# A fifth pair of seven products per gate and up block, a first block in the same form, and part of the weight sums on GpSimd

## The chip, the core and the metric

The kernel runs on one core of a Trainium2 chip. Its engines have a queue of instructions each and run beside each other: TensorE (PE in the profile; its weight loads are PEld), VectorE (DVE), ScalarE (ACT), GpSimd (POOL) and SyncE (SP), which here only issues loads. An instruction waits on semaphores, and everything behind it on its engine waits with it. The metric is the time of one execution in microseconds; the median of several runs is compared.

## What is computed

One layer of a hybrid block for 256 tokens of width 2048, in float32: differential attention and a Conformer convolution side by side, an output projection, then a SwiGLU feed-forward network. The change is in the second half:

```
h  = h + mixed @ w_out                      # 2048 x 2048
hn = rms_norm(h, norm2_g)
a  = hn @ w_gate                            # 2048 x 5632
bu = hn @ w_up                              # 2048 x 5632
h  = h + (silu(a) * bu) @ w_down            # 5632 x 2048
```

`rms_norm` divides each token's row by its root mean square and multiplies by a gain for each column.

## The kernel before

**Three products for one.** Float32 accuracy is made of the faster fp32r matmuls: an operand x is split into `hi` (x rounded, by ScalarE) and `lo` (x - hi, by VectorE), and hi·hi + lo·hi + hi·lo are added up in PSUM. Weights are split as they arrive: a *chunk* is two k-tiles (128 rows each) of 512 columns. `load_chunk` (SP) fetches it into a `raw` buffer, `round_chunk` casts it to `whi`, `split_chunk` makes `wlo` on VectorE. For some chunks (`BY_DMA`) `wlo` is made without VectorE: ScalarE writes -hi and GpSimd issues a DMA that adds the raw weights to it. With tokens in two halves of 128, a chunk takes 2 x 2 x 3 = 12 matmuls of 128x512.

**Seven products for eight.** The FFN's gate and up matrices share their left operand, so a *pair* of k-tiles, two token halves and the two matrices form a 2x2 by 2x2 block product, which a Winograd-like scheme does in seven products: 21 matmuls instead of 24. It costs sums. Of the activations, once: `make_forms` builds seven `forms` (`fhi`, `flo`). Of the weights, for every pair: `round_pair` makes four sums `t` (tile `wt`, three VectorE instructions, L1049 to L1051) and casts the raw weights, `split_pair` casts the sums (L1055) and makes the remainders `wlb` (L1058, 1536 columns) and `wlt` (L1059, 2048 columns). Of the results, once a block: `bank_sums` (L1186 to L1193) adds up the seven PSUM banks when the block's last pair is multiplied, and `block_done` (L1209, L1214) adds the last two when the block is, and multiplies silu(gate) by up. In the profile's names `q` is a PSUM bank, `sum` what is made of it, `wb` a pair's raw weights, `ps_a`, `ahi`, `alo` the transposed result.

**The blocks.** The 5632 hidden columns are 11 blocks of 512. Block 0 is computed with plain chunks, gate and then up, since the activations' forms are made beside it; blocks 1 to 10 have four pairs (NS = 4) and four chunks each of gate and up. Blocks come in groups of 4, 4 and 3 (`FGROUPS`), and after each group a `down_pass` in two halves multiplies its hidden columns by `w_down`, with pairs of its own and forms made by `make_down_forms` (tiles `dsums`, `dlo`, `dls`).

**What sets the order.** The program is emitted chunk by chunk. `ORDER` says in which order a block's units stand: s is a pair, g a gate chunk, u an up chunk. `run_chunks` rounds units three ahead of the one multiplied and splits two ahead (`HI_AHEAD`, `LO_AHEAD`). Between units it resumes generators (`resume`), such as `products_done`, which runs the bank sums, so these stand on VectorE between the remainders of units to come. Buffers bound how far ahead the engines run: `RAW_BUFS` = 5 for `raw`, two for `wb`, `wh`, `wlb` and `wlt`, three for `whi` and `wlo`, one for `wt`. The eight PSUM banks of a block are all that there are.

## Time and profile before

| | |
|---|---|
| runs | 1032.35, 1032.80, 1032.89 us; median 1032.8 |
| span of the profiled execution, first to last instruction | 1030.8 us |
| instructions | 13034, among them 4642 matmuls |
| mean granted TensorE clock | 1.000 |
| loads and stores | 238.64 MB, 232 GB/s |
| VectorE, casts' remainders L335 / L1059 / L1058 | 250.4 / 139.8 / 106.8 us |
| ScalarE, casts L326 / L1055 / L1052 | 264.2 / 116.8 / 89.8 us |
| DMAs issued by GpSimd for `wlo` | 48, 7.1 us to landing |

Of the profiled execution only its span is given; it stands beside a median that is 2.0 us above it. A row of a timeline has the start in the span, the length, the engine, line and operation, out<-in, and in brackets the idle time before it and what ended that. A row of a group has the count, the busy time, the mean of one in ns, and the idle time. A row of a window has its stretch, and for PE, PEld, DVE, ACT and POOL the busy time and count, then the clock.

### The profile page before, as it was taken

What the parts mean: (1) busy time and instruction counts of PE and PEld (TensorE: products, weight loads), DVE (VectorE), ACT (ScalarE), POOL (GpSimd) and SP (SyncE); (2) the same over time, 40 slices, a digit from 0 to 9 for tenths busy, and PEclk for the clock granted to TensorE, in tenths of its full rate; (3) what the DMA queues carried; (4) which work ended last, traced back from release to release, by engine and by line L of the source; (5) the groups of instructions that cost most, each with busy time, mean ns of one, the idle gap of its engine ahead of it and who ended that gap; (6) DMA issues with size and microseconds to landing.
All of it is one profiled execution on the core that took longest, in us unless ns stands there. A gap on an engine that the chain in (4) does not pass through costs nothing.

```text
span 1030.8 us, 13034 instructions
## 1 busy us (share of the span) xinstructions
PE 1025.7 (100%) x4642; PEld 849.4 (82%) x4642; DVE 929.2 (90%) x1128; ACT 643.4 (62%) x786; POOL 102.7 (10%) x146
## 2 busy tenths in 40 slices
PE   9999999999999999999999999999999999999998
PEld 8888888888888888888888888888888888888887
DVE  6899999999765699999999898989999989889998
ACT  7644656665756675676666556667757556657562
POOL 0300112111000000100102101101001111010020
PEclk9999999999999999999999999999999999999999
DMA  9757555544466677997989799889798979897776
GB/s 338 254 194 258 190 184 164 158 169 166 141 215 214 197 262 222 282 265 210 254 259 272 251 257 270 258 234 262 228 269 255 285 207 283 247 267 218 226 200 174
DMA packets 116448, 238.64 MB, mean 232 GB/s; under 512 B 7840, under 2 KB 9120, under 8 KB 116384
## 3 DMA queue, kind: packets, MB, share of 16 engines
q1 hardware_dynamic: 105216, 203.58, 59.3%
q0 software_dynamic: 10880, 34.08, 17.0%
q8 instruction: 36, 0.59, 0.2%
q14 instruction: 28, 0.23, 0.1%
q10 hardware_dynamic: 288, 0.16, 0.1%
HBM read 204.24 MB, written 9.44 MB: 207 GB/s over the span
## 4 chain that ended last, share of the span: by engine, by line
PE 100%; POOL 0%; DVE 0%; issue 0%; POOLq 0%
PE acc L365 11%; PE acc L366 11%; PE acc L371 11%; PE q L1097 11%; PE q L1103 11%; PE q L1098 11%; PE q L1078 9%; PE q L1077 9%; PE q L1076 9%; PE ps_a L898 1%; PE ps_s L712 1%; PE ps_o L782 1%; PE ps_warm L164 0%; PE ps_h L846 0%; PE ps_qk L693 0%; PE ps_at L802 0%
## 5 line engine op out<-in xcount | busy, mean ns | idle before, releaser
L326 ACT CAST whi<-raw 128x1024 fp32r<-128x1024 f32 (+1 forms) x256 | 264.2, 1043 | 143.8 <-PE acc L366 86.6
L335 DVE TENSOR_TENSOR wlo<-raw,whi 128x1024 fp32r<-128x1024 f32 (+1 forms) x208 | 250.4, 1214 | 38.2 <-ACT whi L326 38.0
L1055 ACT CAST wh<-wt 128x2048 fp32r<-128x2048 f32 x61 | 116.8, 1915 | 109.9 <-DVE wt L1051 109.7
L1059 DVE TENSOR_TENSOR wlt<-wt,wh 128x2048 fp32r<-128x2048 f32 x61 | 139.8, 2291 | 19.8 <-ACT wh L1055 19.7
L1097 PE MATMUL q<-whi,chi 128*128 128x512 f32 x320 | 125.2, 391 | 0.0
L1098 PE MATMUL q<-whi,clo 128*128 128x512 f32 x320 | 124.6, 389 | 0.0
L365 PE MATMUL acc<-whi,xhi 128*128 128x512 f32 x312 | 124.1, 398 | 0.0
L366 PE MATMUL acc<-whi,xlo 128*128 128x512 f32 x312 | 122.2, 392 | 0.0
L1076 PE MATMUL q<-wh,fhi 128*128 128x512 f32 x280 | 109.8, 392 | 0.0
L1077 PE MATMUL q<-wh,flo 128*128 128x512 f32 x280 | 109.0, 389 | 0.0
L1058 DVE TENSOR_TENSOR wlb<-wb,wh 128x1536 fp32r<-128x1536 f32 x61 | 106.8, 1751 | 1.0 <-ACT wh L1052 1.0
L572 DVE SCALAR_TENSOR_TENSOR y<-upad,cw,y 128x256 f32<-128x256 f32 x240 | 101.6, 490 | 0.0
L330 POOL DMA_DIRECT2D wlo<-raw x48 | 41.5, 865 | 555.7 <-ACT wlo L329 286.3
L1052 ACT CAST wh<-wb 128x1536 fp32r<-128x1536 f32 x61 | 89.8, 1472 | 1.0 <-DMA wb<-in_w_down_dram 1.0
L1103 PE MATMUL q<-wlo,chi 128*128 128x512 f32 x320 | 85.7, 390 | 0.0
L371 PE MATMUL acc<-wlo,xhi 128*128 128x512 f32 x312 | 85.2, 394 | 0.0
L1049 DVE TENSOR_TENSOR wt<-wb 128x1024 f32<-128x1024 f32 x61 | 74.4, 1220 | 0.0
L1097 PE MATMUL q<-whi,ahi 128*128 128x512 f32 x182 | 71.0, 390 | 0.0
L1098 PE MATMUL q<-whi,alo 128*128 128x512 f32 x182 | 70.9, 389 | 0.0
L1103 PEld LDWEIGHTS q<-wlo,chi 128*128 128x128 f32 x320 | 60.0, 188 | 12.7 <-DMA wlo<-raw 0.3
L1097 PEld LDWEIGHTS q<-whi,chi 128*128 128x128 f32 x320 | 60.1, 188 | 12.3
L1098 PEld LDWEIGHTS q<-whi,clo 128*128 128x128 f32 x320 | 60.1, 188 | 12.2
(260 smaller groups left out, 1850.5 us busy)
## 6 DMA issues: line engine op xcount, KB each, us to landing
raw<-in_w_in_dram SPq DMA_DIRECT2D x78, 512.0 KB, 4.6
raw<-in_w_gate_dram SPq DMA_DIRECT2D x48, 512.0 KB, 5.0
raw<-in_w_up_dram SPq DMA_DIRECT2D x48, 512.0 KB, 5.3
wlo<-raw POOLq DMA_DIRECT2D x48, 512.0 KB, 7.1
raw<-in_w_down_dram SPq DMA_DIRECT2D x46, 512.0 KB, 6.2
wb<-in_w_down_dram SPq DMA_DIRECT2D x42, 512.0 KB, 5.9
wb<-in_w_up_dram SPq DMA_DIRECT2D x40, 512.0 KB, 4.4
wb<-in_w_gate_dram SPq DMA_DIRECT2D x40, 512.0 KB, 5.5
```

What stands on the lines that cost most here:

```text
L326: act.copy(c["hi"], c["raw"])
L335: dve.tensor_tensor(c["lo"], c["raw"], c["hi"].bitcast(F32), ALU.subtract)
L365: pe.matmul(ps[m], xhi[:, ms], hi[:, j, :], start=c["first"] and j == 0, stop=False)
L366: pe.matmul(ps[m], xlo[:, ms], hi[:, j, :], start=False, stop=False)
L371: pe.matmul(ps[m], xhi[:, ms], lo[:, j, :], start=False, stop=c["last"] and j == nk - 1)
L1055: act.copy(c["hi"][:, :SUMMED], c["t"])
L1059: dve.tensor_tensor(lot, c["t"], c["hi"][:, :SUMMED].bitcast(F32), ALU.subtract)
L1076: pe.matmul(ps, hi, c["hi"][:, w], start=bool(first), stop=False)
L1077: pe.matmul(ps, lo, c["hi"][:, w], start=False, stop=False)
L1097: pe.matmul(ps, xs[i][0][:, ms], hi[:, i, :], start=i == 0 and bool(c["first"].get(qs[m])), stop=False)
L1098: pe.matmul(ps, xs[i][1][:, ms], hi[:, i, :], start=False, stop=False)
L1103: pe.matmul(sum_bank(c, qs[m]), xs[i][0][:, ms], lo[:, i, :], start=False, stop=i == 1 and bool(c["last"].get(qs[m])))
```

## The change

- **A fifth pair.** `PAIRS` lists pairs of k-tiles: (0,8), (1,9), (2,10), (3,11) and now (4,5). Blocks 1 to 10 use all five, and three chunks each of gate and up are left (tiles 6, 7, 12 to 15). `ORDER` becomes "sgsgsgsusuu", for block 1 "gsgsgssusuu".
- **Block 0** takes the form of the others with four pairs, in the order "gugusgsgssuu"; the plain code for it (`silu_done`, `up_done`) goes. Its PSUM pools are exchanged (`swap`).
- **Row factors later.** The activations are no longer multiplied by the rows' factor `rstd2` ahead of the forms (four VectorE instructions and two transposes go); it is applied to the gate's sums, by the Silu's scale and by one more copy (`products_done`). So `make_forms` starts after the third of the four output-projection blocks, and `out_done` writes `rows` and the remaining tiles' `chi` and `clo` straight from PSUM.
- **GpSimd sums.** The three instructions for a pair's sums `t` are in `first_sums(c, engine)`. At the end of `bank_sums`, `sums_aside` lets GpSimd make them for the next pair that is not rounded yet, if its raw weights were loaded and the pair ahead of it is split. `bank_sums` also releases one bank earlier.
- **Halves.** `split_pair` casts `t` in two instructions of 1024 columns and makes `wlt` in two.
- `RAW_BUFS` goes from 5 to 4. Memory is laid out in new pools (`keep`, `late`, `edge`).

```diff
-RAW_BUFS = 5
+RAW_BUFS = 4
...
-NS = 4
-REST = [k for k in range(KD) if k % HK >= NS]
+PAIRS = [(0, 8), (1, 9), (2, 10), (3, 11), (4, 5)]
+NS = len(PAIRS)
+REST = [k for k in range(KD) if not any(k in p for p in PAIRS)]
...
-BY_DMA = dict(g=TWOS[:2], u=TWOS[1::2])
-ORDER = "sggsggsuusuu"
-FIRST_ORDER = "gsggsgsuusuu"
+BY_DMA = dict(g=TWOS[:2], u=TWOS[1:])
+ORDER = "sgsgsgsusuu"
+ORDERS = {1: "gsgsgssusuu"}
+NS0 = 4
+TWOS0 = [*PAIRS[NS0:], *TWOS]
+ORDER0 = "gugusgsgssuu"
+DOWN_ORDER = "sggsggsuusuu"
...
     def round_pair(c):
...
-        c["t"] = t = fp.tile([P, 4, N], F32, tag="wt", name="wt")
         c["hi"] = fp.tile([P, 7, N], F32R, tag="wh", name="wh", bufs=2)
-        dve.tensor_tensor(t[:, 2:4], b[:, 1:3], b[:, 0:1].to_broadcast([P, 2, N]), ALU.subtract)
-        dve.tensor_tensor(t[:, 1], b[:, 1], t[:, 3], ALU.add)
-        dve.tensor_tensor(t[:, 0], t[:, 1], b[:, 3], ALU.subtract)
+        if "t" not in c:
+            first_sums(c, dve)
         act.copy(c["hi"][:, SUMMED:], b[:, 1:])
 
+    def first_sums(c, engine):
+        b = c["b"]
+        c["t"] = t = ffn["pool"].tile([P, 4, N], F32, tag="wt", name="wt")
+        engine.tensor_tensor(t[:, 2:4], b[:, 1:3], b[:, 0:1].to_broadcast([P, 2, N]), ALU.subtract)
+        engine.tensor_tensor(t[:, 1], b[:, 1], t[:, 3], ALU.add)
+        engine.tensor_tensor(t[:, 0], t[:, 1], b[:, 3], ALU.subtract)
+
+    def sums_aside():
+        pairs = [c for c in chunks if c.get("kind") == "s"]
+        n = next((n for n, c in enumerate(pairs) if not c.get("rounded")), None)
+        if n and "b" in pairs[n] and "lo" in pairs[n - 1]:
+            first_sums(pairs[n], pool)
+
     def split_pair(c):
-        act.copy(c["hi"][:, :SUMMED], c["t"])
...
-        dve.tensor_tensor(lob, c["b"][:, 1:], c["hi"][:, SUMMED:].bitcast(F32), ALU.subtract)
-        dve.tensor_tensor(lot, c["t"], c["hi"][:, :SUMMED].bitcast(F32), ALU.subtract)
+        for i in (2, 0):
+            act.copy(hi[:, i : i + 2], t[:, i : i + 2])
+        rest(lob, b[:, 1:], hi[:, SUMMED:])
+        for i in (2, 0):
+            rest(lot[:, i : i + 2], t[:, i : i + 2], hi[:, i : i + 2])
...
         dve.tensor_tensor(u3, q[Q7], u2, ALU.add)
+        dve.tensor_tensor(w1, q[Q2], w1, ALU.add)
         dve.tensor_tensor(w4, q[Q5], u3, ALU.add)
         dve.tensor_tensor(u2, q[Q5], u2, ALU.add)
-        dve.tensor_tensor(w1, q[Q2], w1, ALU.add)
         dve.tensor_tensor(u3, q[Q4], u3, ALU.add)
+        sums_aside()
...
-        for t in g:
-            act.activation(t, t, AF.Silu)
+        for m, t in enumerate(g):
+            act.activation(t, t, AF.Silu, scale=rstd2[m])
+            act.activation(t, t, AF.Copy, scale=rstd2[m])
```

VectorE from the last bank sum of block 1 to pair 2 of block 2, before (`sum`, `q`: the block's sums and banks; `wt`, `wlb`, `wlt`: pair 2's sums and remainders):

```order
L1193 TENSOR_TENSOR sum_4002<-q_3709,sum_4002 128x512
L1209 TENSOR_TENSOR sum_4001<-q_3760,sum_4001 128x512
L1209 TENSOR_TENSOR sum_4003<-q_3918,sum_4003 128x512
L1214 TENSOR_TENSOR sum_4001<-sum_4001,sum_4000 128x512
L1214 TENSOR_TENSOR sum_4003<-sum_4003,sum_4002 128x512
L1049 TENSOR_TENSOR wt<-wb 128x1024
L1050 TENSOR_TENSOR wt<-wb,wt 128x512
L1051 TENSOR_TENSOR wt<-wt,wb 128x512
L1058 TENSOR_TENSOR wlb<-wb,wh 128x1536
L1059 TENSOR_TENSOR wlt<-wt,wh 128x2048
```

The same place now:

```order
L1199 TENSOR_TENSOR sum_4007<-q_3723,sum_4007 128x512
L1217 TENSOR_TENSOR sum_4006<-q_3775,sum_4006 128x512
L1217 TENSOR_TENSOR sum_4008<-q_3942,sum_4008 128x512
L1222 TENSOR_TENSOR sum_4006<-sum_4006,sum_4005 128x512
L1222 TENSOR_TENSOR sum_4008<-sum_4008,sum_4007 128x512
L1064 TENSOR_TENSOR wlb<-wb,wh 128x1536
L1064 TENSOR_TENSOR wlt<-wt,wh 128x1024 x2
```

Pair 2's three sums have left VectorE at this place, and `wlt` is made in halves. They stand on GpSimd, among the DMAs that it issues for `wlo`; from the row factor on, its queue reads:

```order
L234 TENSOR_TENSOR rstd_145<-rsq,neghalf 128x2
L340 DMA wlo<-raw 128x1024 x6
L1040 TENSOR_TENSOR wt<-wb 128x1024
L1041 TENSOR_TENSOR wt<-wb,wt 128x512
L1042 TENSOR_TENSOR wt<-wt,wb 128x512
L340 DMA wlo<-raw 128x1024 x4
```

The first set belongs to pair 2 of block 2; there are 14 in all, for pair 2 of blocks 2 to 10 and of five halves of down passes. Before, no sums stood there. VectorE from the last bank sums of block 0 to pair 2 of block 1, now:

```order
L1198 TENSOR_TENSOR sum_3664<-q_3490,sum_3664 128x512
L1199 TENSOR_TENSOR sum_3665<-q_3346,sum_3665 128x512
L1064 TENSOR_TENSOR wlb<-wb,wh 128x1536
L1064 TENSOR_TENSOR wlt<-wt,wh 128x1024 x2
L1217 TENSOR_TENSOR sum_3664<-q_3386,sum_3664 128x512
L1217 TENSOR_TENSOR sum_3666<-q_3389,sum_3666 128x512
L1222 TENSOR_TENSOR sum_3664<-sum_3664,sum_3663 128x512
L1222 TENSOR_TENSOR sum_3666<-sum_3666,sum_3665 128x512
L345 TENSOR_TENSOR wlo<-raw,whi 128x1024
L1040 TENSOR_TENSOR wt<-wb 128x1024
L1041 TENSOR_TENSOR wt<-wb,wt 128x512
L1042 TENSOR_TENSOR wt<-wt,wb 128x512
```

Here pair 1's remainders stand behind the bank sums and ahead of the closing sums, and pair 2's sums stay on VectorE. Before, block 0 had no bank sums, and in their place stood two products of silu and up (L883).

## The prediction

> **What bounds the kernel now.** I read the shares of the engines first, then the slices, then the chain of waits.

> ```profile
> PE 1025.7 (100%) x4642; PEld 849.4 (82%) x4642; DVE 929.2 (90%) x1128; ACT 643.4 (62%) x786; POOL 102.7 (10%) x146
> PE   9999999999999999999999999999999999999998
> DVE  6899999999765699999999898989999989889998
> PE 100%; POOL 0%; DVE 0%; issue 0%; POOLq 0%
> ```

> TensorE is busy in every slice and is the whole chain: nothing else ever ends last. So a matmul removed is time removed, as long as the matmuls left are still fed in time. VectorE is the engine to fear, at nine tenths from slice 17 on, the half with the FFN.

> What a matmul costs, and the length of a block, from the timeline of TensorE around block 2, and from the windows:

> ```profile
> 456.62 0.39 PE L1077 MATMUL q<-wh,flo 128*128 128x512 f32 x1
> ...
> 461.16 0.39 PE L1097 MATMUL q<-whi,chi 128*128 128x512 f32 x1
> ...
> 466.60 0.39 PE L1076 MATMUL q<-wh,fhi 128*128 128x512 f32 x1
> 466.60:508.00 41.40, 41.40 (x188) 34.31 (x187) 39.87 (x41) 27.95 (x27) 3.05 (x4) 1.00 0.80 231
> ```

> Between the first two rows lie 20 starts: 4.54 / 20 = 0.227 us a matmul. A pair (21) holds TensorE 4.77 us, a chunk of two whole k-tiles (12) 2.72. At 461.16 the pairs of the block are done (its "half"), at 466.60 the next block begins: two chunks, 5.44 us, during which VectorE sums the banks. The window is one block, 180 matmuls and 8 transposes: (41.40 - 40.86) = 0.5 us for the transposes, at a clock of 1.00.

> What VectorE does across that seam, from its timeline (start, length):

> ```profile
> 457.14 1.75 DVE L1058 TENSOR_TENSOR wlb<-wb,wh 128x1536 fp32r<-128x1536 f32 x1
> 458.81 2.29 DVE L1059 TENSOR_TENSOR wlt<-wt,wh 128x2048 fp32r<-128x2048 f32 x1
> 461.13 0.69 DVE L1188 TENSOR_TENSOR sum<-q,sum 128x512 f32<-128x512 f32 x1
> 461.93 0.69 DVE L1189 TENSOR_TENSOR sum<-q,sum 128x512 f32<-128x512 f32 x1
> ...
> 465.12 0.68 DVE L958 TENSOR_TENSOR dsums<-raw_act,dsums 128x512 f32<-128x512 f32 x1
> 466.34 1.29 DVE L1209 TENSOR_TENSOR sum<-q,sum 128x512 f32<-128x512 f32 x2 [0.54 <-PE q L1103]
> 467.55 1.29 DVE L1214 TENSOR_TENSOR sum<-sum,sum 128x512 f32<-128x512 f32 x2
> 468.75 1.22 DVE L1049 TENSOR_TENSOR wt<-wb 128x1024 f32<-128x1024 f32 x1
> 470.00 0.69 DVE L1050 TENSOR_TENSOR wt<-wb,wt 128x512 f32<-128x512 f32 x1
> 470.73 0.69 DVE L1051 TENSOR_TENSOR wt<-wt,wb 128x512 f32<-128x512 f32 x1
> 471.34 0.68 DVE L962 TENSOR_TENSOR dlo<-raw_act,dhi 128x512 fp32r<-128x512 f32 x1
> 471.94 1.75 DVE L1058 TENSOR_TENSOR wlb<-wb,wh 128x1536 fp32r<-128x1536 f32 x1
> 474.43 2.29 DVE L1059 TENSOR_TENSOR wlt<-wt,wh 128x2048 fp32r<-128x2048 f32 x1 [0.73 <-ACT wh L1055]
> ...
> 477.23 2.35 DVE L335 TENSOR_TENSOR wlo<-raw,whi 128x1024 fp32r<-128x1024 f32 x2
> 479.50 1.22 DVE L1049 TENSOR_TENSOR wt<-wb 128x1024 f32<-128x1024 f32 x1
> 477.72 0.39 PE L1078 MATMUL q<-wlt,fhi 128*128 128x512 f32 x1
> ```

> Starts overlap lengths, so I price by start to start: six bank sums 4.0 us (461.13 to 465.12), the four sums that close a block 2.4, a pair's three first sums 2.6 (468.75 to 471.34), its wlb 1.67, a 1024-wide remainder 1.13 (two in 2.27), a small op 0.6. The last two rows give the spare time: pair 2's remainders end at 476.72, TensorE wants the first at 477.72. **One microsecond of lead**, because VectorE must wait for the block's end (466.34) before it can start pair 2. It rebuilds the lead later in the block.

> **The change part by part.**

> 1. Matmuls. Block 0: 192 become 180. Ten blocks: 180 become 177. 12 + 30 = 42 fewer, 42 x 0.227 = 9.5 us; two transposes of the row factors go too, 0.1, and I count 9.7.

> 2. VectorE's new load. Without GpSimd a pair costs 2.6 + 1.67 + 2 x 1.13 = 6.5 us; one whose sums GpSimd made costs 3.9. In a block with five pairs TensorE takes 177 x 0.227 + 0.5 = 40.7 us. VectorE between two sets of bank sums, from the instructions in their order: 46.4 for block 0 to 1 (4.0 bank sums, 2.4 closing, 3.9 pair 1's remainders, five pairs of 6.5, three chunks' remainders 3.4), 40.5 to block 2, 44.8 to 3 (two chunks' remainders, four pairs of 6.5, one of 3.9, ten small ops), about 37 and 34 (down), 39.8, 38.7, 40.5, 44.8 (to 7), and under 40.7 from there. So it is above TensorE in three places only, by 5.7, 4.1 and 4.1, 13.9 us together: that is the loss if no lead carries over; if all of it carries, the loss is nothing. Both ends are kept.

> 3. Block 1, step by step, from block 0's end on TensorE = 0 (its half is -5.4). VectorE: bank sums to -1.4, pair 1's remainders (they stand behind the bank sums now) to 2.5, wanted at 2.72 + 0.45 = 3.2: in time. The closing sums to 4.9, one chunk's remainder 6.0, pair 2 to 12.6. TensorE, in the order g s g s, wants it at 2.72 + 4.77 + 2.72 + 0.45 + 0.25 (transposes) = 10.9: **1.7 us stall**. Pair 3 to 20.2, wanted at 20.3. Pair 4 follows pair 3 with no chunk between (order ...ss...): ready at 26.8, wanted at 25.1, **1.7**. Pair 5: 0.2. Sum 3.6 us.

> 4. A steady block (2, 5, 6, 8, 9), start = 0. Closing sums end at 2.1 (at 3.1 in block 2, entered 1 us late). Pair 2, summed by GpSimd, 6.1, wanted at 4.77 + 2.72 + 0.45 = 7.9. Pair 3 12.6 against 15.4, pair 4 20.3 against 22.9, pair 5 28 to 29.5 against 30.4. No stall.

> 5. Blocks 3 and 7 carry ten more small ops, 6 us: in block 3, entered 1.3 us late, pair 4 is ready at 24.1 against 23.4 and pair 5 0.7 late again, 1.4 us in all; in block 7, entered nearly on time, 0.5. Then the bank sums begin 4.7 us after the half; TensorE takes the banks back one by one, the last of them 4 us into the next block, so that wait stays off its path. Block 10 and the six down passes: nothing. Losses: 3.6 + 1.4 + 0.5 = 5.5 us.

> 6. Casts in halves. The second remainder now needs only one half-cast; this row and the 0.73 above show the wait that goes:

> ```profile
> L1059 DVE TENSOR_TENSOR wlt<-wt,wh 128x2048 fp32r<-128x2048 f32 x61 | 139.8, 2291 | 19.8 <-ACT wh L1055 19.7
> ```

> 19.8 / 61 = 0.3 us a pair, which I left out of the 6.5. If the wait stayed, block 1 would lose about 1.3 us more, and blocks 3 and 7 as much each: 4 us.

> 7. GpSimd's sums. No row shows one of this size; the nearest are small, with VectorE's beside them:

> ```profile
> 36.40 0.46 POOL L200 TENSOR_TENSOR gcsq<-rt,gb 128x128 f32<-128x128 f32 x1
> 36.82 0.32 POOL L201 TENSOR_TENSOR gcsq<-rt,gb 128x64 f32<-128x64 f32 x1
> 37.10 1.30 POOL L202 TENSOR_TENSOR gcsq<-rt,gb 128x64 f32<-128x64 f32 x1
> 39.07 0.32 POOL L202 TENSOR_TENSOR gcsq<-rt,gb 128x64 f32<-128x64 f32 x1
> 36.90 1.32 DVE L335 TENSOR_TENSOR wlo<-raw,whi 128x1024 fp32r<-128x1024 f32 x1 [1.71 <-ACT whi L326]
> ```

> Starts are 0.42 apart for 128 columns and 0.28 for 64: 2.2 ns a column and 0.14. 1024 + 512 + 512 columns: an estimate of 4.9 us, against 2.6 on VectorE as the lower end. It begins when pair 1's remainders end, about the half, and so ends 0.5 us ahead of the block's end: hidden, since pair 2's remainders start 2.1 after it. If that cover goes, see the second rival. Queued behind these sums on GpSimd stand the DMA issues of the next wlo; the first has 14 us until its matmul.

> The same rows show a clash. L202 takes 1.30 beside a VectorE op on two SBUF tensors that ends at 38.22, and 0.32 alone; the VectorE op takes 0.1 longer than the 1.22 at 479.50. Beside ops that read PSUM there is none:

> ```profile
> 126.08 1.01 POOL L671 TENSOR_TENSOR fk<-ssq,neghalf 128x4 f32<-128x4 f32 x1
> 126.46 0.41 DVE L682 TENSOR_TENSOR t<-acc,gcsk 128x256 f32<-128x256 f32 x1
> L671 POOL TENSOR_TENSOR fk<-ssq,neghalf 128x4 f32<-128x4 f32 x4 | 4.0, 1009 | 0.3
> ```

> L671 keeps its mean. The bank sums read PSUM, so the sums on GpSimd and those on VectorE lie side by side; I take no clash in the sum. [...]

> 8. The rest. The forms of the hidden rows are made under the last output-projection block and under block 0's four whole chunks (4 x 2.72 us of cover); a miss costs at most one chunk, 2.7. Loads keep their bytes: 28 chunks of one matrix become 28 halves of pairs on SP's queue. Four raw buffers instead of five: a block now has 6 such chunks, not 8.

> ```profile
> raw<-in_w_gate_dram SPq DMA_DIRECT2D x48, 512.0 KB, 5.0
> ```

> A load of 5.0 us against the four chunks (10.9 us) that four buffers hold: nothing, with up to 2 us in the opening, where loads come as fast as they are used. ACT gets some 45 us more at 62%: off the path.

> Sum: 1030.8 - 9.7 + 5.5 = 1026.6 us of span. The runs' median, 1032.8, is 2.0 above the span; with that, **1028.6 us**.

> **Rivals.** (a) Every surplus is absorbed: 1032.8 - 9.7 = 1023.1. For it: in the profile of before VectorE has leads that grow inside each block and TensorE never waits. Against: block 1's stall comes after a wait that empties the lead.

> (b) The sums on GpSimd slip from under the bank sums. The mechanism is the clash above; the place is pair 2 of the nine blocks 2 to 10; it decides when the last sum ends later than 4.0 us after the block's start (7.9 less the 3.9 of pair 2's remainders, which then wait behind the sums), 4.5 us later than I think. Each further microsecond costs nine; if VectorE waits all 4.9 us from 2.1 on, pair 2 is ready at 10.9 against 7.9: 9 x 3.0 = 27, 1056. I price it at 1.5 us a block: 1028.6 + 13.5 = 1042. [...]

> (c) No lead carries: 1032.8 - 9.7 + 13.9 = 1037.0, slower. It holds if VectorE waits at each block for the half and the end as now, and pays its surplus on top. Against: block 2's 40.5 is under 40.7, and the down passes return 4 to 6 us each.

> (d) Nothing is gained since the losses equal 9.7: 1032.8, between forecast and (c). That GpSimd's sums would not be taken is ruled out by the order, which has 14 sets of them.

> **How the numbers follow.** Forecast 0.50, with its own range of 1026 to 1031.5; (a) 0.18; (b) 0.10; (c) 0.12; (d) 0.10. The predicted time is the forecast's. The range takes in (a) and (c): 1022.5 to 1037. A measurement can tell 0.2%, 2.1 us: faster is below 1030.7. Faster: 0.18 and 0.42 of the forecast's half, 0.60; slower: (b) and most of (c), 0.20; same: 0.20.

> **What would show it.** Right: the idle time of TensorE stands before matmuls on wlt (pairs 2 and 4) of block 1, 3 to 4 us, and some 2 us in blocks 3 and 7, ended by VectorE; GpSimd's first sum lasts about 2.4 us and starts beside the bank sums. Step 1 is right if TensorE has 42 matmuls fewer at 0.227. Wrong: TensorE idle before pair 2 of every block, or GpSimd rows far above 2.4; or a chain of waits that goes through ACT or a DMA, which the sum holds off the path.

## The result, and the profile after

The changed kernel takes **1041.7 us** (median of four runs, 1039.2 to 1045.9) against 1032.6: ratio 1.0092, 95% interval 1.0079 to 1.0106. It is slower by 9 us where 4 less were forecast, and above the range. The profiled execution took 1043.9 us, 2.2 above the median, its span 1042.1; the losses below are those of this one execution. From the page, the engines and the chain; then the view of waits for TensorE (waiting line, what it waited for, us in total, times, longest):

```profile
PE 1023.0 (98%) x4598; PEld 842.1 (81%) x4598; DVE 950.9 (91%) x1202; ACT 689.5 (66%) x876; POOL 180.2 (17%) x191
PE 13%; DMA 1%; DVE 0%; issue 0%
```

```profile
PE q L1107 <- DMA wlo<-raw: 6.7, 7, 1.9
PE ps_h L867 <- DVE h L849: 2.9, 2, 2.7
PE q L1082 <- DVE wlt L1064: 2.0, 2, 1.3
PE ps_warm L174 <- POOL neghalf L168: 1.4, 1, 1.4
PE acc L408 <- ACT whi L336: 1.2, 1, 1.2
PE acc L381 <- DVE wlo L345: 1.1, 1, 1.1
```

44 instructions of TensorE are gone, the 42 matmuls and two transposes, so the gain of step 1 is there. What ate it is new: the largest wait is for a DMA, on remainders made beside VectorE (`wlo`, L1107), which the prediction had named as a sign that it is wrong; only the third line is the wait that was forecast. A wait's row counts the engine's empty time; what TensorE loses is a little more. Taking every start-to-start of two matmuls, less 0.227 us, I get 10.3 us lost in the span of before and 30.4 now. The 20.1 us more are:

| lost by TensorE, us | before | now |
|---|---|---|
| remainders by DMA (L1107) | 0 | 8.0 |
| transposes of h ahead of block 0 (L867) | 0 | 3.3 |
| a remainder ahead of block 0 (L381) | 0 | 1.3 |
| matmuls at half clock | 0 | 3.3 |
| pairs 2 and 4 of block 1 (L1082) | 0 | 2.3 |
| the first 230 us | 5.4 | 6.1 |
| the rest, 0.02 to 0.3 us each | 4.9 | 6.1 |

1030.8 - 9.6 + 20.1 = 1041.3, near the 1042.1 measured.

**The start of block 0.** VectorE, then TensorE, timelines:

```profile
341.56 1.22 DVE L1040 TENSOR_TENSOR wt<-wb 128x1024 f32<-128x1024 f32 x1
342.81 0.69 DVE L1041 TENSOR_TENSOR wt<-wb,wt 128x512 f32<-128x512 f32 x1
343.54 0.69 DVE L1042 TENSOR_TENSOR wt<-wt,wb 128x512 f32<-128x512 f32 x1
344.14 1.22 DVE L345 TENSOR_TENSOR wlo<-raw,whi 128x1024 fp32r<-128x1024 f32 x1
345.28 1.28 DVE L849 TENSOR_TENSOR h<-h,acc 128x512 f32<-128x512 f32 x2
```

```profile
342.28 1.07 PE L1107 MATMUL q<-wlo,hhi 128*128 128x512 f32 x4
346.02 0.33 PE L867 MATMUL ps_h<-ident,h 128*128 128x128 f32 x1 [2.67 <-DVE h L849]
```

The first pair's sums (L1040 to L1042) are emitted one step ahead of the additions to h (L849) that the transposes wait for. And TensorE's gap has an aftermath. The windows of this gap, behind it, and behind the longest wait on a DMA (stretch; PE, PEld, DVE, ACT, POOL; the clock; then the DMA engines' share and GB/s):

```profile
343.00:346.40 3.40, 0.68 (x3) 0.14 (x1) 3.37 (x5) 0.41 (x1) 0.14 (x1) 1.00 0.68 247
346.90:350.30 3.40, 3.40 (x11) 2.72 (x10) 2.17 (x5) 2.24 (x5) 1.40 (x3) 0.50 0.80 293
449.30:452.70 3.40, 3.40 (x9) 2.63 (x8) 3.40 (x4) 1.99 (x2) 0.00 (x0) 0.50 0.93 304
```

For 3.4 us behind each wait the granted clock is 0.50 and a matmul takes 0.427 instead of 0.227 us: 8 matmuls, 1.6 us lost twice.

**A steady block.** Block 2, whose second gate chunk has its remainder by DMA. ScalarE, GpSimd, then VectorE and SyncE's queue, timelines:

```profile
432.74 0.73 ACT L1209 ACTIVATE sum<-sum,rstd 128x512 f32<-128x512 f32 x1
433.37 1.99 ACT L1057 CAST wh<-wt 128x1024 fp32r<-128x1024 f32 x2
435.27 1.05 ACT L336 CAST whi<-raw 128x1024 fp32r<-128x1024 f32 x1
436.22 1.06 ACT L339 ACTIVATE wlo<-raw 128x1024 fp32r<-128x1024 f32 x1
```

```profile
428.50 2.73 POOL L1040 TENSOR_TENSOR wt<-wb 128x1024 f32<-128x1024 f32 x1
431.31 1.30 POOL L1041 TENSOR_TENSOR wt<-wb,wt 128x512 f32<-128x512 f32 x1
432.69 1.30 POOL L1042 TENSOR_TENSOR wt<-wt,wb 128x512 f32<-128x512 f32 x1
437.80 0.88 POOL L340 DMA_DIRECT2D wlo<-raw  x1 [3.82 <-ACT raw_act L913]
```

```profile
435.06 1.75 DVE L1064 TENSOR_TENSOR wlb<-wb,wh 128x1536 fp32r<-128x1536 f32 x1
436.93 0.37 SPq L1022 DMA_DIRECT2D wb<-in_w_up_dram  x1
437.34 0.47 SPq L1022 DMA_DIRECT2D wb<-in_w_gate_dram  x1
```

And TensorE, whose matmul ahead of the last row starts at 446.19:

```profile
446.19 0.39 PE L1102 MATMUL q<-whi,clo 128*128 128x512 f32 x1
448.49 1.44 PE L1107 MATMUL q<-wlo,chi 128*128 128x512 f32 x4 [1.91 <-DMA wlo<-raw]
```

It wants this `wlo` at 446.4 and gets it at 448.49. GpSimd's queue is not what delays it: it stood idle for 3.82 us. The copy on ScalarE (L339) stands behind the two half-casts of pair 2's sums (L1057), and these behind the scaling of the gate's sums (L1209). ScalarE does not wait for GpSimd here: the sums are done at 433.99, and the second half-cast starts at 434.32 without idle time before it. And the transfer enters 0.5 to 0.9 us behind a pair's loads, the first of which starts 0.12 us after VectorE's `wlb` (done at 436.81) has set their buffer free. The DMA view of 436.9 to 438.2 gives the times to landing:

```profile
wb<-in_w_up_dram SPq DMA_DIRECT2D x1, 512.0 KB, 3.8
wb<-in_w_gate_dram SPq DMA_DIRECT2D x1, 512.0 KB, 5.3
wlo<-raw POOLq DMA_DIRECT2D x1, 512.0 KB, 10.6
raw<-in_w_up_dram SPq DMA_DIRECT2D x1, 512.0 KB, 9.5
```

10.6 us, against a median of 7.1 before. It moves nothing for the first 4.6 us: in the DMA view of 438.0 to 442.4 the only queue with packets is SyncE's (packets, MB, share of the 16 DMA engines):

```profile
q1 hardware_dynamic: 596, 1.15, 94.7%
```

Over 9 us there were 3 of 48 such transfers before, and 14 of 51 now.

### The profile page after: what moved, and what is told of

Read it like the earlier page. It is cut to its first block, busy times and chain, and to the rows that moved or that the text cites. A ratio compares the mean times of both kernels' runs of the same rounds, so it can differ in the third digit from the quotient of the medians.

```text
span 1042.1 us, 13141 instructions
## 1 busy us (share of the span) xinstructions
PE 1023.0 (98%) x4598; PEld 842.1 (81%) x4598; DVE 950.9 (91%) x1202; ACT 689.5 (66%) x876; POOL 180.2 (17%) x191
## 5 line engine op out<-in xcount | busy, mean ns | idle before, releaser
L336 ACT CAST whi<-raw 128x1024 fp32r<-128x1024 f32 (+1 forms) x228 | 237.6, 1044 | 133.6 <-PE acc L376 66.0
L345 DVE TENSOR_TENSOR wlo<-raw,whi 128x1024 fp32r<-128x1024 f32 (+1 forms) x177 | 214.9, 1218 | 46.7 <-ACT whi L336 42.3
L1057 ACT CAST wh<-wt 128x1024 fp32r<-128x1024 f32 x150 | 155.0, 1052 | 83.8 <-DVE wt L1040 56.9
L1064 DVE TENSOR_TENSOR wlt<-wt,wh 128x1024 fp32r<-128x1024 f32 x150 | 176.5, 1218 | 0.7 <-ACT wh L1057 0.7
L1080 PE MATMUL q<-wh,fhi 128*128 128x512 f32 x378 | 148.0, 392 | 0.0
L1081 PE MATMUL q<-wh,flo 128*128 128x512 f32 x378 | 147.6, 390 | 0.0
L1064 DVE TENSOR_TENSOR wlb<-wb,wh 128x1536 fp32r<-128x1536 f32 x75 | 131.3, 1751 | 5.7 <-ACT wh L1035 5.6
L1082 PE MATMUL q<-wlt,fhi 128*128 128x512 f32 x216 | 85.0, 393 | 2.0 <-DVE wlt L1064 2.0
L381 PE MATMUL acc<-wlo,xhi 128*128 128x512 f32 x312 | 84.9, 393 | 0.0
L1081 PEld LDWEIGHTS q<-wh,flo 128*128 128x128 f32 x378 | 71.4, 189 | 15.0
L1080 PEld LDWEIGHTS q<-wh,fhi 128*128 128x128 f32 x378 | 71.4, 189 | 14.7
L1040 DVE TENSOR_TENSOR wt<-wb 128x1024 f32<-128x1024 f32 x61 | 74.4, 1220 | 4.2 <-DMA wb<-in_w_gate_dram 2.7
L1107 PE MATMUL q<-wlo,chi 128*128 128x512 f32 x264 | 71.7, 393 | 3.3 <-DMA wlo<-raw 3.3
## 6 DMA issues: line engine op xcount, KB each, us to landing
raw<-in_w_in_dram SPq DMA_DIRECT2D x78, 512.0 KB, 3.9
wb<-in_w_up_dram SPq DMA_DIRECT2D x54, 512.0 KB, 4.2
wb<-in_w_gate_dram SPq DMA_DIRECT2D x54, 512.0 KB, 6.0
wlo<-raw POOLq DMA_DIRECT2D x51, 512.0 KB, 7.4
raw<-in_w_down_dram SPq DMA_DIRECT2D x46, 512.0 KB, 6.0
wb<-in_w_down_dram SPq DMA_DIRECT2D x42, 512.0 KB, 5.8
raw<-in_w_gate_dram SPq DMA_DIRECT2D x34, 512.0 KB, 4.4
raw<-in_w_up_dram SPq DMA_DIRECT2D x34, 512.0 KB, 7.2
```

The costliest lines, as they stand in the source:

```text
L336: act.copy(c["hi"], c["raw"])
L345: dve.tensor_tensor(c["lo"], c["raw"], c["hi"].bitcast(F32), ALU.subtract)
L1057: act.copy(hi[:, i : i + 2], t[:, i : i + 2])
L1064: dve.tensor_tensor(lo, raw, h.bitcast(F32), ALU.subtract)
L1080: pe.matmul(ps, hi, c["hi"][:, w], start=bool(first), stop=False)
L1081: pe.matmul(ps, lo, c["hi"][:, w], start=False, stop=False)
```

## The experiments

Theories: A, GpSimd's sums themselves make the remainders late; B and C, the loads of five pairs come in lumps and a transfer that enters behind a lump is late; and, for the whole, that VectorE has no lead left, so that what is mended at one place is lost at the next. Times are medians; before was 1032.6 or 1032.7 beside every one. Of the views of waits only the lines that bear on the argument are shown.

**1. Sums back on VectorE**, in `sums_aside`:

```diff
-            first_sums(pairs[n], pool)
+            pass
```

> The changed kernel with the 14 sets of GpSimd sums put back on VectorE; nothing else differs. Theory A (the sums on GpSimd make the remainders by DMA late: the copies on ScalarE stand behind casts that wait for GpSimd, and the DMA issues stand behind the sums): the flights of 9.5 to 11 us of the wlo transfers that are issued beside or right after a set go back to about 7, the idle time before the matmuls on such a wlo goes from 6.7 us and more to under 1.5; in exchange VectorE has 14 x 2.6 = 36 us more, some 2.4 us a block above TensorE in nine blocks, so up to 20 us stand before matmuls on wlt: 1040 to 1052 us. Theory B (the transfers are late because the loads of five pairs with four raw buffers come in bunches, whoever makes the sums): flights stay at 9.5 to 11 where loads are bunched and the waits on wlo stay at 6 us or more beside the wlt stalls: 1048 to 1058.

1054.8 us (ratio 1.0214, 1.02 to 1.0227), in the range of theory B. Its waits:

```profile
PE q L1082 <- DVE wlt L1064: 7.2, 13, 1.3
PE q L1107 <- DMA wlo<-raw: 3.0, 4, 1.8
PE ps_h L867 <- DVE h L849: 2.9, 2, 2.7
PE ps_a L906 <- DVE sum L1222: 1.7, 7, 0.3
PE q L1080 <- DVE sum L1217: 1.6, 2, 0.8
```

GpSimd's sums are worth 13 us to this kernel. The flights separate: the first gate chunk's stay long (9.7 and 10.3 us in blocks 2 and 3, as with the sums on GpSimd), the second's fall from 10.6 and 9.1 to 6.2 and 6.0, and there the transfer entered at 437.16, 0.6 us ahead of the pair's loads (437.77). Counted from the first of block 1's bank sums, the transfer enters at 10.0 us here and at 9.7 in the change, the loads at 10.6 here and at 8.9 in the change. So GpSimd's sums do not hold this transfer up. They end VectorE's `wlb` 1.7 us sooner, and with it the loads come in front. Here the long flight goes with the order of entry: 10.6 us behind the pair's loads, 6.2 ahead of them.

**2. The first pair later**, in `run_chunks`:

```diff
-            if t == first - 1:
-                chunks[pairs[0]]["round"](chunks[pairs[0]])
```

> The changed kernel without the step that makes the first pair's sums and casts ahead of the last output-projection chunk's multiplication; they then come two chunks later, by the usual lead. Theory A (the three first sums, 2.6 us on VectorE, stand ahead of the last two additions to h, so the transposes of h come 2.8 us late, and the gap makes the granted clock fall to 0.5 for 3.4 us, 1.6 us more): the gap of 3.06 us before the transposes falls under 0.8 and the halved clock goes with it, -3.5 to -4.5 us: about 1037.5. Rival B (the additions are late because of the four remainders of whole chunks and the forms ahead of them, or the transposes wait for the last matmul anyway): the gap stays above 2 us, 1041 to 1042. Rival C (the first pair is then late itself): a new wait of 2 to 4 us before the first matmul on wh or wlt in block 0, 1040 to 1043.

1042.5 us (1.008 to 1.0107): no gain. The gap of 3.06 us is 0.47 and the half clock is gone, as A said; 1.5 us come back as a first wait on `wlt` in block 0 (C), and 1.7 on `wlt` in blocks 4 and 8.

**3. Fewer remainders by DMA:**

```diff
-BY_DMA = dict(g=TWOS[:2], u=TWOS[1:])
+BY_DMA = dict(g=TWOS[:1], u=TWOS[1:])
-DOWN_BY_DMA = {4: (dict(g=(0, 1), u=(1,)),) * 2, ...
+DOWN_BY_DMA = {4: (dict(g=(0,), u=(1,)),) * 2, ...
```

> The changed kernel with the second gate chunk's remainder made by VectorE instead of by DMA, in the seven blocks that had it and in four down passes (11 remainders of 1.13 us more on VectorE); GpSimd keeps its sums. Theory A (what was lost in the steady blocks is the lateness of these very transfers: 2.07, 1.56, 0.40, 1.17, 1.71, 0.37 and 0.50 us of waits and about 1.5 us of the halved clock after the longest): the waits on a wlo that lands by DMA fall to under 1.5 us in all and new waits on wlt are under 3: 1032 to 1036. Rival B (VectorE has no room for them): waits on wlt and wlo of VectorE take their place, 1040 to 1046. Rival C (the next transfer in the queue is late instead, the first gate chunk's or an up chunk's): the waits on wlo by DMA stay above 4 us, 1039 to 1042.

1046.4 us (1.0118 to 1.0146), rival B, a little above its range: the waits on DMA fell from 6.7 to 2.3 us, those on `wlt` rose from 2.0 to 7.4. Eleven remainders, 12 us, were more than VectorE had.

**4. Four raw buffers alone**, in the kernel before:

```diff
-RAW_BUFS = 5
+RAW_BUFS = 4
```

> The kernel before with four raw buffers instead of five, nothing else. Theory A (the stall of 1.3 us in the opening before the first whole chunks comes from the missing buffer; from there on four are enough): about 1.3 us slower, 1033.5 to 1034.5, with the idle time before the matmuls on whi at about 10.5 us. Theory B (four buffers also make the loads come in bunches and the remainders by DMA late): 1036 to 1040, with flights of wlo of 9 us and more. Theory C: no difference, 1032.3 to 1033.

1035.1 us (1.0015 to 1.0036), 2.5 slower, between the theories: 0.8 us more lost in the opening, where the forecast had "up to 2", and a wait of 1.4 on `wlt` in block 1 that was not foreseen and whose cause stays open. Flights stay at a median of 7.1.

**5. The chunk first**, where GpSimd made the sums:

```diff
+            aside = j < i and chunks[j].get("aside")
-            while j < min(i, t + 1 + lo_lead):
+            while j < min(i, t + 1 + lo_lead) and not aside:
                 split_next()
```

> The changed kernel with one exchange on ScalarE: where a pair's sums were made by GpSimd, the next chunk's cast and copy (and so its transfer) come ahead of that pair's two half-casts instead of behind them. Theory C (a remainder by DMA is late when it is put in just behind a pair's 1 MB of loads, which start the moment VectorE's wlb frees the buffer: 437.80 against 436.93, flight 10.6 us; with the sums on VectorE it went in 0.6 us ahead of them, flight 6.2): the second gate chunk's transfer is now put in some 2 us sooner, ahead of the loads, its flight falls from 9 to 10.6 us to 6 to 7 in blocks 2, 3, 5, 6, 7, 9 and 10, and the waits of 2.07, 1.17 and 0.50 us on it and the halved clock behind the first go: 1036 to 1038; the waits in the two down passes (3.9 us) stay. Theory D (the flight is long because GpSimd's sums or the total of the loads slow every transfer in that stretch): flights stay above 9 and the issue 2 us sooner gains 2 us at most, 1039.5 to 1041.5. Rival E (the half-casts are now late): waits on wlt of some 2 us in these blocks, 1041 or more.

The DMA view of the same place, 432.5 to 437:

```profile
wlo<-raw POOLq DMA_DIRECT2D x1, 512.0 KB, 5.7
wb<-in_w_up_dram SPq DMA_DIRECT2D x1, 512.0 KB, 6.0
wb<-in_w_gate_dram SPq DMA_DIRECT2D x1, 512.0 KB, 6.9
raw<-in_w_up_dram SPq DMA_DIRECT2D x1, 512.0 KB, 7.3
```

The transfer enters at 433.03, the loads at 434.06: 5.7 instead of 10.6 us, and the waits of blocks 2, 5 and 9 are gone. VectorE's `wlb` and `wlt` ran during this flight too (432.19 to 436.21), so they are not what makes one long. Theory C holds. But the median is 1042.3 (1.0078 to 1.0109; the profiled run 1039.8, others up to 1045.1): waits on `wlt` rose from 2.3 to 5.1, in block 3 above all.

**6. No gate remainders by DMA in the second pass:**

```diff
-DOWN_BY_DMA = {4: (dict(g=(0, 1), u=(1,)),) * 2, ...
+DOWN_BY_DMA = {4: (dict(g=(0, 1), u=(1,)), dict(g=(), u=(1,))), ...
```

> The changed kernel with the two gate remainders in the second pass of the first two down projections made by VectorE instead of by DMA (4 remainders of 1.13 us). These are the transfers with waits of 1.56, 0.40, 1.71 and 0.37 us: one is put in behind 1.5 MB of loads (flight 10.8 us), the other stands 4.1 us behind GpSimd's sums. Theory A (VectorE has room here, it stands idle for 0.5 and 1.8 us behind the seam): -3 to -4 us, 1037.5 to 1038.5. Rival B (VectorE is full and the lead of the pair behind is lost, as in the run with fewer remainders by DMA): waits on wlo and wlt of VectorE of 1 to 2 us a pass take their place, 1040 to 1043.

1043.6 us (1.0098 to 1.0125). The expectation had the place wrong: the late transfers stand in the first pass (matmuls at 526.09 and 529.34 in the change), so the waits stayed (7.6 us). It says nothing on A or B.

**7. GpSimd's sums alone**, in the kernel before (`first_sums` and `sums_aside` as in the change):

```diff
         dve.tensor_tensor(u3, q[Q4], u3, ALU.add)
+        sums_aside()
```

> The kernel before with the 14 sets of sums of a pair's first stage on GpSimd, nothing else: four pairs a block, five raw buffers, casts whole. Theory A (TensorE never waits in the FFN of before, so VectorE's 36 us are worth nothing; and the second gate chunk of a block, that stands behind the pair on ScalarE, has its transfer put in later): 1033 to 1037, with waits on wlo by DMA of 1 to 4 us. Theory B (no harm and no gain): 1032.3 to 1033. Theory C (a gain): under 1031.

1033.9 us (1.0005 to 1.0023), 1.3 slower. VectorE's busy time fell from 929.2 to 902.4 and no remainder was late; one bank sum in the last pass cost 1.2. In the kernel before, whose view of waits shows TensorE waiting for VectorE nowhere, 26.8 us less on VectorE gained nothing.

**8. Block 0 with one more remainder by DMA**, besides 2:

```diff
-                   dict(g=TWOS0[2:], u=TWOS0[2:3]), swap=not j)
+                   dict(g=TWOS0[2:], u=TWOS0[1:3]), swap=not j)
```

> The changed kernel with the first pair's sums behind the additions to h (as in the run before this one on the same point), and, beside that, block 0's second up remainder by DMA instead of VectorE. Theory A (what that step alone lost was the first wait on wlt in block 0, 1.47 us, since VectorE had the pair's sums 2.6 us later; 1.13 us less on VectorE take most of it away): the gap before the transposes of h is 0.5 us, the wait on wlt in block 0 under 0.6: 1037 to 1039. Theory B (the gain at the seam is given back later, since block 1 starts with less lead on VectorE): the waits on wlt in block 1 grow from 2.3 to 3 us or more, 1040 to 1042. Theory C (the added transfer is itself late, behind the first loads of pairs): a wait on that wlo of 1 us or more.

1041.8 us (1.0079 to 1.0105): the transfers of block 0 were late by 2.7 and 0.8 us, theory C.

**9. No fifth pair;** the rest of the change stays:

```diff
-PAIRS = [(0, 8), (1, 9), (2, 10), (3, 11), (4, 5)]
+PAIRS = [(0, 8), (1, 9), (2, 10), (3, 11)]
-BY_DMA = dict(g=TWOS[:2], u=TWOS[1:])
+BY_DMA = dict(g=TWOS[:2], u=TWOS[1::2])
-ORDER = "sgsgsgsusuu"
-ORDERS = {1: "gsgsgssusuu"}
+ORDER = "sggsggsuusuu"
+ORDERS = {1: "gsggsgsuusuu"}
```

> The changed kernel with four pairs in the ten blocks again (their orders and their remainders by DMA as before), but with all the rest of the change: block 0 by pairs, sums on GpSimd, casts in halves, four raw buffers. TensorE has 30 matmuls more than the changed kernel, 6.8 us. Theory A (the waits on wlo by DMA, the halved clock behind them and the waits on wlt in block 1 come from the fifth pair: it puts 1 MB of loads where 512 KB stood and takes VectorE's lead): those 8.0, 1.6 and 2.3 us go, the 6.3 us at the start of block 0 stay: 1041.7 + 6.8 - 11.9 = 1036.6, between 1035 and 1038. Theory B (GpSimd's sums, the halves and the four buffers make these waits by themselves): the waits stay, 1045 to 1049. Theory C (the part that is left is a gain by itself, 12 matmuls fewer than before): under 1032.

1037.3 us (1.0032 to 1.0059; all five runs between 1037.0 and 1037.7). This is within 0.7 us of theory A. The page's engines and the waits:

```profile
PE 1024.5 (99%) x4628; PEld 847.9 (82%) x4628; DVE 905.9 (88%) x1162; ACT 670.0 (65%) x864; POOL 180.6 (17%) x191
```

```profile
PE ps_h L867 <- DVE h L849: 2.7, 2, 2.5
PE q L1107 <- DMA wlo<-raw: 1.7, 1, 1.7
```

**As the change has it, the fifth pair is a loss of 4.4 us:** it saves 30 matmuls, 6.8 us of TensorE, and costs 950.9 - 905.9 = 45 us of VectorE, 4.5 a block for 0.7. Flights over 9 us fall from 14 to 2 of 51. The waits on `wlt` are gone.

**10. The chunk first after every pair** that isn't followed by another:

```diff
-            while j < min(i, t + 1 + lo_lead):
+            while j < min(i, t + 1 + lo_lead) and (
+                    chunks[j].get("kind") != "s" or i >= n or chunks[i].get("kind") == "s"):
                 split_next()
```

> The changed kernel with the chunk that follows a pair cast, and its transfer put in, ahead of the half-casts of that pair, now after every pair and not only where GpSimd made the sums. Theory C (order of entry: a 512 KB transfer behind a pair's loads takes 10 us, ahead of them 6): flights over 9 us fall from 14 of 51 to under 6, the waits on wlo by DMA from 4.7 us (in the run with the exchange in 14 places) to under 2, in the down passes too; 1036 to 1039 in executions without a halved clock. Rival D (the transfers in the down passes are held up by the copies or by GpSimd): waits of 3 to 4 us on wlo there stay, 1039 to 1042. Rival E: half-casts late, waits on wlt up by 3 us or more.

1038.3 us (1.0049 to 1.0075), 3.3 better than the change. Waits:

```profile
PE q L1083 <- DVE wlt L1065: 4.3, 5, 1.4
PE ps_h L868 <- DVE h L850: 2.8, 2, 2.6
PE acc L381 <- DVE wlo L345: 1.0, 1, 1.0
PE q L1102 <- DVE sum L1200: 1.0, 1, 1.0
```

No line for a DMA is left: theory C, in the first down pass too. The late transfers and the half clock behind them had cost 9.6 us; 2.8 came back as waits on `wlt`, 1.7 on bank sums in the last pass. That leaves 5.1, and between the two profiled executions lie 5.6 (spans 1042.1 and 1036.5); between the medians it is 3.3.

**11, 12. Combined.** 10 and 2 together, and GpSimd's sums later in the first pass of a down projection; then also block 1 with four pairs:

```diff
-                   [... for p, k in enumerate(PAIRS[: NS if j else NS0])],
+                   [... for p, k in enumerate(PAIRS[: NS if j > 1 else NS0])],
-ORDERS = {1: "gsgsgssusuu"}
+ORDERS = {1: "gsggsgsuusuu"}
```

> The changed kernel with three edits: chunks ahead of half-casts after every pair; the first pair's sums behind the additions to h; in the first pass of a down projection GpSimd's sums two steps later, so that the second gate remainder's transfer is put in ahead of them. If the losses are those named (at the start of block 0 the gap and the halved clock, 4.4 us, less a wait of 1.5 on wlt; waits on wlo by DMA 8.0 and the halved clock 1.6 behind them): 1041.7 - 2.9 - 8 to 9.6 = 1029 to 1031, faster than both kernels. If the time given back at one place is lost at the next, since VectorE is above nine tenths busy: 1033 to 1038.

> The same three edits, and block 1 with four pairs in the order it had before (3 matmuls more, 0.7 us; VectorE has 5 us less to do between block 0 and block 2). If the waits on wlt in blocks 0 and 1 come from VectorE's demand of 46.4 us there: 2.3 us less waits in block 1, 1.6 us better than the run without: 1027.5 to 1029.5 where that one gives 1029 to 1031. If the lead carries on to the first down pass, another 1 us on the waits on wlt there. Rival: the loss moves to the next place where VectorE is above TensorE (block 3), equal times or 0.7 us worse.

1041.5 us (1.0069 to 1.0094) and 1037.8 (1.0042 to 1.0067). The first is above the 1038 that its expectation allowed at most; the second gains more on it than the 1.6 expected. Combined:

```profile
PE q L1081 <- DVE wlt L1063: 8.7, 9, 1.5
PE q L1106 <- DMA wlo<-raw: 0.6, 2, 0.3
```

The waits on DMA are mended and what they had cost comes back as waits on VectorE. Moving the sums missed its point, since those ahead of the late transfer are issued with block 3's bank sums, not in the pass, and it did harm: run 16 is run 12 without this one edit, and 3.1 us faster (1034.7). So part of what the combination lost is the edit's own. Four pairs in block 1 give 3.7 us for 3 matmuls more.

**13 to 15. Without the fifth pair, mended.** 9 with 2; with 10 besides; with five raw buffers besides.

> The changed kernel without the fifth pair, and without the early step that makes the first pair's sums ahead of the last output-projection chunk. Theory A (the start of block 0 is most of the 7.3 us that this kernel has lost on the sum of its matmuls: 3.1 us before the transposes of h, 1.7 of halved clock, 1.9 on a wlo by DMA in block 0): the gap and the halved clock go, a wait on wlt of up to 1.5 us in block 0 comes in their place: 1033.5 to 1035. Rival B (given back at the next place): 1036 to 1037.5.

> As the last, and chunks cast and put in ahead of the half-casts of the pair that they follow. Theory A (the wait of 1.9 us on the wlo by DMA in block 0 comes from its entry behind the first pairs' loads, flight 10.4 us): its flight falls under 8 and 1.5 to 2 us go, 1032 to 1033.5. Rival B (VectorE then waits for the half-casts): waits on wlt of 1 us or more, 1033.5 to 1036.

> As the last, with five raw buffers, which fit without the fifth pair's forms. Before with four buffers was 2.5 us slower than with five. Theory A (the same holds here): 1 to 2.5 us faster than the last, 1030 to 1032, faster than before by 1 to 2.5 us, the worth of block 0's 12 matmuls. Rival B (the fourth buffer is worth nothing once no load of a pair stands in front of a transfer): equal to the last.

1034.8 us (1.0015 to 1.0032), 1036.1 (1.0024 to 1.0048), 1034.2 (1.0006 to 1.0023). The start of block 0 was 2.5 us, and a wait of 1.5 on `wlt` stays there. Putting the chunk first gains nothing here (1.3 us slower, with intervals that overlap): neither theory, since the wait on `wlt` stays at 1.3; 1.4 us on bank sums in the last pass are new. The fifth buffer gives back 1.8.

**16 to 18. With the fifth pair, mended.** 10 and 2, block 1 with four pairs; then besides two of the output projection's last remainders by DMA (in 17 without the exchange of 10 in the last pass); then only one:

```diff
+    for c in (chunks[-3], chunks[-1]):
+        c["by_dma"] = True
```

> The changed kernel with its fifth pair in nine blocks (block 1 has four), the first pair's sums behind the additions to h, and chunks ahead of half-casts; GpSimd's sums stay where the change has them. Theory A (with transfers in time and block 1 relieved, what is left are waits on wlt in the down passes, about 2 us, and at the start 3 us): 1032 to 1035, near before: the nine pairs' 27 matmuls, 6.1 us, pay for the waits that they bring. Theory B (VectorE is full: what is won at block 1 is lost in the passes and blocks 5 and 9): 1036 to 1039.

> As the run with five pairs mended, and two edits more: the third from last and the last remainder of the output projection by DMA (VectorE has 2.3 us less to do just ahead of block 0), and no exchange of chunks and half-casts in the last pass. Theory A (VectorE's queue ahead of block 0 is what delays the remainder there, the additions to h and the first pair: 1.2, 0.7 and 1.9 us; the exchange in the last pass is what delays the bank sums, 1.7 us): 3 to 4.5 us less waits: 1030 to 1032, faster than before. Theory B (the transfers are late there, or the lead is used up elsewhere): 1033 to 1035.

> As five_mended, and only the last remainder of the output projection by DMA (1.13 us less on VectorE between the forms and the first pair of block 0); the exchange stands in the last pass too. Theory A (VectorE's queue sets the additions to h and the first pair): the waits before the transposes of h, 0.7, and before the first wlt in block 0, 1.5, shrink by 1 to 1.8 us in all, 1033 to 1033.7, near before. Theory B (the lead won is lost again in the passes): 1034.3 to 1035.5. Theory C (the added transfer is late): a wait of 1 us or more on it, over 1035.

1034.7 us (1.0009 to 1.0026), 1038.3 (1.0036 to 1.0063), 1035.5 (1.0016 to 1.004). The first is 7 us better than the change and equal to the mended kernel without a fifth pair (run 13); beside run 14, which has the same mends, it is 1.4 us faster, with intervals that overlap. So the fifth pair in nine blocks, 6.1 us less of TensorE, is no loss once the other places are mended, and little or no gain. The other two were lost to late transfers, 4.4 and 2.9 us, with a half clock behind each. **No version beat the kernel before.**

## Why the prediction was wrong

1. *Matmuls.* Right: 42 fewer, at 0.227 us wherever the clock is full.

2. *VectorE's load.* Right. From one set of bank sums to the next VectorE was busy for 46.0 us (block 0 to 1), 41.0 (to 2), 44.9 (to 3) and 44.2 (to 7), where 46.4, 40.5, 44.8 and 44.8 were forecast. Over the whole execution it has 21.7 us more.

3. *Block 1*, 1.7, 1.7 and 0.2 forecast: 0.9, 1.4 and 0 measured, on the lines named.

4, 5. *Steady blocks, and blocks 3 and 7.* On VectorE right. In the profile of the change there is no wait on `wlt` in block 3, since the late transfers hold TensorE back there first. Where they are mended (run 10) it waits 0.86 and 0.66 us in block 3 and 0.58 in block 7: 1.5 and 0.6, where 1.4 and 0.5 were forecast. So two waits hid one another, and the sum of VectorE's step was nearly the whole truth once the DMA's was gone.

6. *Halves.* Right: of the 19.8 us that `wlt` waited for ScalarE, 0.7 are left. The group in the page:

```profile
L1064 DVE TENSOR_TENSOR wlt<-wt,wh 128x1024 fp32r<-128x1024 f32 x150 | 176.5, 1218 | 0.7 <-ACT wh L1057 0.7
```

7. *GpSimd's sums.* From the groups of its lines:

```profile
L1040 POOL TENSOR_TENSOR wt<-wb 128x1024 f32<-128x1024 f32 x14 | 39.2, 2798 | 28.6 <-DVE wlt L1064 28.5
L1042 POOL TENSOR_TENSOR wt<-wt,wb 128x512 f32<-128x512 f32 x14 | 20.6, 1469 | 1.1
L1041 POOL TENSOR_TENSOR wt<-wb,wt 128x512 f32<-128x512 f32 x14 | 18.2, 1297 | 1.1
```

5.6 us for 4.9, from the half on, under the bank sums; pair 2's remainders were not late. The clash of the second rival shows where the sums outlast the bank sums: the closing pair of operations in block 2, beside GpSimd's last sum (432.69 to 433.99), takes 2.07 us where it took 1.29, and 1.28 in run 1, which has no such sums. So rival (b), whose 1042 is what was measured, is not what happened; the match of the number is chance. ScalarE's casts waited for GpSimd at two of the 14 sets, in blocks 4 and 8, 8.6 us of ScalarE's time, and TensorE did not wait there:

```profile
ACT wh L1057 <- POOL wt L1042: 5.1, 2, 2.6
ACT wh L1057 <- POOL wt L1040: 3.5, 2, 1.8
```

**The step that failed** is this one's last sentence, that the DMA issues queued behind the sums have 14 us until the first matmul, together with "Loads keep their bytes" in step 8: they put the transfers at nothing. In block 2 the second gate chunk's transfer entered 8.6 us before its matmul, which the median flight of 7.1 would still have met; it flew 10.6, since VectorE, rid of the sums, had set 1 MB of loads free in front of it. Late transfers cost 8.0 us in all, and 1.6 of half clock. GpSimd's own queue delayed a transfer too, in the first pass: its copy on ScalarE was done at 517.1 and it entered behind the sums at 521.25. TensorE lost 0.4 us there, and in run 1, without the sums, that transfer entered 2.2 us behind the one ahead of it instead of 6.0, and flew 11.1 us instead of 8.0.

8. *The rest.* "Loads keep their bytes" was true and not the point: they keep them in lumps of 1 MB, ahead of or behind a transfer that has little to spare. How little could have been read in the trace of before: 9 of the 48 transfers landed less than 1.5 us ahead of the weight load that waited for them, though the median was 3.2 us (now 28 of 51, median 1.2). "ACT off the path" fell with it: in block 2 ScalarE worked without a break from 431.98 us on, and the copy that the transfer needs came out of its queue at 437.28. "A miss costs at most one chunk, 2.7" was 3.3 + 1.3 us ahead of block 0, and 1.6 of half clock: the step emitted ahead of the additions to h is part of the change (`run_chunks`), and its price was not worked out.

In the sum: 5.5 us of losses forecast, 20.1 found; of these 2.3 are waits on VectorE in block 1, 6.2 the start of block 0 with its half clock, 9.6 late transfers with theirs. What the runs leave open is the wait in block 1 with four raw buffers, why a transfer behind the loads moves nothing for over 4 us, what block 0's form and the halves are worth alone, and how far the spread of the changed kernel's runs (6.7 us, against 0.5 before) comes from order of entry and how far from the half clock; the runs at 0.998 and 1.000 mean clock took 1039.2 and 1039.5, those at 0.997 and 0.995 1043.9 and 1045.9.

## What to carry to other kernels

When a change takes work off an engine, ask what that engine will now do sooner, and what this sets off: here VectorE freed a buffer 1.7 us sooner, 1 MB of loads entered ahead of a transfer, and TensorE waited for that transfer. Before trading one engine's time for another's, divide: 4.5 us of an engine at nine tenths for 0.7 us of the bound lost 4.4 us as written and was worth next to nothing with the other places mended. And read how much spare time each transfer has, not only the median flight: here, with a median of 1.2 us to spare, half a microsecond either way decided, 10.6 us of flight for a transfer that entered 0.5 us behind the loads and 6.2 for one 0.6 ahead of them.
